# A hybrid decoder layer on one core: transfers that wait moved from SP's queue to POOL's, the residual spilled by chunks, and the fourth weight sum made last

## The chip, the core and the metric

The kernel runs on one core of a Trainium2 chip. Its time is the device time of one execution in microseconds (us); of several executions the median counts. The engines are TensorE (PE in the profile; its weight loads are PEld), VectorE (DVE), ScalarE (ACT), GpSimd (POOL) and SyncE (SP). Each engine works off its own instructions in order. DMAs are issued by SP (rows "SPq"), POOL ("POOLq") and ACT ("ACTq"); their packets appear in the profile under queue q1 (SP), q0 (POOL) and q10 (ACT), and all are carried by the core's 16 DMA engines.

## What is computed

One layer (DEPTH 1) of a decoder trunk on 512 positions of width 2048, in float32:

```
proj = rmsnorm(h) @ w_in                              # 2048 x 6672
ya = spatial gating MLP, 4 heads x 128;  yb = gated short convolution, 4 groups x 128
yc = gated DeltaNet, 8 heads x 128: short conv, silu, l2norm, a triangular solve by chunks, a scan
h = h + concat[ya, yb, yc] @ w_o
h = h + square(relu(rmsnorm(h) @ w_ff1)) @ w_ff2      # 2048 x 8192 and 8192 x 2048
h = h + (p @ w_ple_proj) * sigmoid(rmsnorm(h) @ w_ple_gate)
out = rmsnorm(h)
```

## The kernel before

Every large product is made of three matmuls: each operand is split into a high part (a cast by ACT, L181 and L276) and the rest (a subtraction by DVE, L182 and L277), and high x high, high x low and low x high are summed in PSUM. A weight tile is loaded by SP, split, and multiplied; tiles lie in a ring of SBUF (`place`, RING) and are loaded some slots ahead, since `wload` gives its instructions a high priority. The order of the instructions on each engine is made by a scheduler from such priorities.

The stages, by the time of the profile: the norm of x and the first columns of `w_in` (to 60 us); the spatial gating columns, with the decays of the heads made beside them in `prep` (to 140); eight heads (140 to 640), each with 16 weight loads and the generator `gdn` advanced between matmuls; four groups of the short convolution (to 780); `w_o` in two halves, of which `residual` adds blocks of 512 columns into the residual tiles `hs` (to 960); the up phase, `up_pairwise` for two groups of columns and `up_products` for thirty (to 1630); the down phase, seven calls of `product` (to 2260); gate, projection and final norm.

Up and down phase use fewer products than the plain form, at the price of sums. Of `w_ff2` four sums are made in DRAM, beside all else, by DMAs alone: `presum` yields one piece at a time. For each of 16 steps and each sum q0 to q3, SP copies a block of `w_ff2` to DRAM in four pieces (`copies`, L210), and POOL adds another block, or another sum, to it with accumulating DMAs (`adds`, L219). `count` is called for every weight load and draws pieces from the generator at `pace[1]` loads a piece:

```
def count(n=1):
    pace[0] += n
    while pace[1] and pace[0] >= pace[1]:
        pace[0] -= pace[1]
        next(sums, None)
```

In a head, `gdn` writes the products of k with themselves to DRAM (`at`, L600), reads their diagonal blocks back (`blk`, L602), has POOL invert these in a chain of small products into `tb`, and writes `tb` to DRAM (`td`, L645), from where `T` is read (L656). At its end the head's result `zs` goes to DRAM (`mix`, L733); after the second convolution group all eight are read back in pairs through one buffer `xs` (L795), and split. The residual is spilled before the large weight buffers `wp` take its place (`hsd`, L1032), and reloaded for the down phase (L1047). The up phase writes hidden rows to DRAM (`hd`, L979, issued by POOL), the down phase loads them (L1077) beside `w_ff2` or the sums (L1079).

Of the kernel before, what the change touches and what calls it, by code (L numbers as in the profile page):

```python
# [15 lines left out]
ALU = mybir.AluOpType  # L16
# [3 lines left out]
P = 128  # L20
S = 512
NT = S // P
# [36 lines left out]
def hybrid_block(ctx: ExitStack, tc: tile.TileContext, x, p, norm_mix, w_in, sg_ln_g, sg_ln_b, sg_w,  # L59
# [142 lines left out]
    def pieces(q, st, src):  # L202
        for b in range(2):
            for c in range(0, FW, 512):
                yield qd[q][st][:, b, c:c + 512], src[:, b, c:c + 512]

    def copies(i):
        for q, a, f in ((0, 0, 0), (2, 1, 1), (3, 1, 0), (1, 1, 1)):
            for dst, src in pieces(q, i, w2block(i, a, f)):
                tc.keep_in_program_order(nc.sync.dma_start(dst, src))  # L210
                yield

    def adds(i):
        for q, lag in ((0, 1), (2, 1), (1, 2), (3, 3)):
            st = i - lag
            if 0 <= st < NST:
                other = w2block(st, 0, 1) if lag == 1 else qd[0 if q == 1 else 1][st]
                for dst, src in pieces(q, st, other):
                    tc.keep_in_program_order(nc.gpsimd.dma_start(dst, src, accum_op=ALU.add))  # L219
                    yield  # L220

    def presum():
        for i in range(NST + 3):
            todo = [copies(i)] if i < NST else []
            todo.append(adds(i))
            while todo:
                for gen in list(todo):
                    try:
                        next(gen)
                    except StopIteration:  # L230
                        todo.remove(gen)
                        continue
                    yield
# [136 lines left out]
    pace[1] = 0.9  # L370

# [182 lines left out]
    if True:  # L554
# [32 lines left out]
        def gdn(c):  # L587
# [57 lines left out]
            nc.sync.dma_start(diag(td[h]), tb)  # L645
# [87 lines left out]
            nc.sync.dma_start(mixd[h], zs)  # L733
# [3 lines left out]
        gd = None  # L737
        for h in range(H):
# [42 lines left out]
        for gi in range(4):  # L781
            ps = [pd.tile([P, S], F32, name="d") for _ in range(3)]
            feature_major(col_blocks(w_in, [SC0 + 512 * i + gi * P for i in range(3)]), 3, KD, 2, ps)
            if gi == 1:
# [6 lines left out]
                for h in range(H):  # L791
# [3 lines left out]
                    nc.sync.dma_start(mt, mixd[h])  # L795
# [19 lines left out]
    def chain(*gens):  # L815
        for gen in gens:
            yield from gen
# [59 lines left out]
    def residual(c, ps, pool, nm, ss, g0, scale=None):  # L877
        for tt in range(NT):
            hc = accumulate(tt, c, ps[tt], scale)
            nc.scalar.activation(ps[tt], hc, AF.Square, accum_out=ss[:, tt, c:c + 1])  # L880
# [150 lines left out]
    for tt in range(NT):  # L1031
        nc.sync.dma_start(hsd[tt], hs[tt])  # L1032
# [5 lines left out]
    pace[1] = 1  # L1038
    for g in range(2, NG):
        up_products(g, *((pd, "d"), (pg, "g"))[g % 2])  # L1040
    for _ in sums:
        pass
# [194 lines left out]
```

## Time and profile before

| | |
|---|---|
| time, median of 3 runs (lowest, highest) | 2489.27 us (2488.5, 2491.82) |
| time of the profiled execution | 2482.61 us |
| its span, from the first to the last instruction | 2480.8 us |
| TensorE busy, share of the span | 2399.0 us, 97% |
| DVE, ACT, POOL busy | 60%, 43%, 16% |
| mean granted TensorE clock | 0.984 of full speed |
| moved by DMA | 508.91 MB, 205 GB/s; q1 52.4%, q0 20.7% of the 16 engines |

Durations in this document are from the profiled execution. A share of a DMA queue is the time that its packets took, as a share of all 16 engines over the stretch. A busy TensorE is not one at full speed: its granted clock stands beside the busy time, 1.00 at 2.4 GHz and 0.50 at 1.2 GHz.

### The profile page before, as it was taken

The page shows a single profiled execution, that of the slowest core. Times are in us where ns is not written, and L with a number is a line of the kernel's source. Part 1 is how long each engine was busy: PE and PEld are TensorE (multiplying, and loading weights), DVE is VectorE, ACT ScalarE, POOL GpSimd, SP SyncE. Part 2 cuts the span into 40 slices and gives each one's busy share as a digit, 9 for nine tenths or more (in the row PEclk, how much of TensorE's full clock was granted, in tenths as well). Part 3 has the DMA queues.
Part 4 walks back from the last instruction along what each step waited for, and adds up shares of the span by engine and source line. Part 5 has one row for each costly group of instructions (what it writes and reads, how often), then busy time and mean ns, then how long its engine had stood idle before and what let it go on. Part 6 is the DMA issues. An engine that isn't in the chain of part 4 may idle for free.

```text
span 2480.8 us, 35947 instructions
## 1 busy us (share of the span) xinstructions
PE 2399.0 (97%) x13852; PEld 2110.6 (85%) x13852; DVE 1488.5 (60%) x2047; ACT 1060.7 (43%) x1585; POOL 402.2 (16%) x613
## 2 busy tenths in 40 slices
PE   9999999999979999899999999989999999999998
PEld 8987888888857888899999999968888888888888
DVE  6654444444435357688888888855566565565334
ACT  5343333333323244344444444444444454455333
POOL 1433333333031100121222212310000000000000
PEclk9999999999989999999999999989999999999999
DMA  7976777776698946899889898988777777763333
GB/s 228 251 173 151 162 163 163 164 165 154 146 202 226 249 141 189 248 246 250 238 238 245 241 247 226 220 265 295 239 237 237 241 233 243 235 214 125 100 102 115
DMA packets 350175, 508.91 MB, mean 205 GB/s; under 512 B 38010, under 2 KB 218035, under 8 KB 348083
## 3 DMA queue, kind: packets, MB, share of 16 engines
q1 hardware_dynamic: 302436, 403.58, 52.4%
q0 software_dynamic: 44544, 96.49, 20.7%
q10 hardware_dynamic: 3024, 6.55, 0.8%
q8 instruction: 108, 1.77, 0.3%
q14 instruction: 63, 0.52, 0.1%
HBM read 460.11 MB, written 180.63 MB: 258 GB/s over the span
## 4 chain that ended last, share of the span: by engine, by line
PE 79%; DMA 9%; POOL 4%; DVE 3%; issue 2%; ACT 1%; SPq 1%; POOLq 0%; ACTq 0%; DVEq 0%
PE g L270 7%; PE g L271 7%; PE g L272 7%; PE d L270 7%; PE d L272 7%; PE d L271 7%; PE g L956 4%; PE g L957 4%; PE g L958 4%; PE d L957 4%; PE d L956 4%; PE d L958 4%; PE d L319 4%; PE d L320 4%; PE d L318 4%; DMA wraw<-in_w_in_dram 3%
## 5 line engine op out<-in xcount | busy, mean ns | idle before, releaser
L182 DVE TENSOR_TENSOR wl<-wraw,wh 128x512 fp32r<-128x512 f32 (+3 forms) x336 | 250.4, 748 | 364.6 <-ACT wh L181 356.3
L181 ACT CAST wh<-wraw 128x512 fp32r<-128x512 f32 (+3 forms) x336 | 216.9, 648 | 508.8 <-PE d L320 186.3
L318 PE MATMUL d<-XH,wh 128*128 128x512 f32 x704 | 296.9, 422 | 17.2 <-ACT wh L181 17.2
L319 PE MATMUL d<-XH,wl 128*128 128x512 f32 x704 | 278.8, 396 | 0.2 <-DVE wl L182 0.2
L320 PE MATMUL d<-XL,wh 128*128 128x512 f32 x704 | 278.5, 396 | 0.0
L1011 ACT CAST wh<-wp 128x1024 fp32r<-128x1024 f32 x140 | 147.2, 1051 | 197.5 <-PE g L958 99.3
L1012 DVE TENSOR_TENSOR wl<-wp,wh 128x1024 fp32r<-128x1024 f32 x140 | 170.9, 1221 | 54.8 <-ACT wh L1011 54.7
L277 DVE TENSOR_TENSOR wl<-wraw,wh 128x1024 fp32r<-128x1024 f32 x112 | 137.2, 1225 | 106.8 <-ACT wh L276 106.8
L277 DVE TENSOR_TENSOR r<-xr,r 128x1024 fp32r<-128x1024 f32 x112 | 136.8, 1222 | 77.0 <-ACT r L276 77.0
L276 ACT CAST wh<-wraw 128x1024 fp32r<-128x1024 f32 x112 | 118.2, 1055 | 141.3 <-PE d L272 72.7
L318 PEld LDWEIGHTS d<-XH,wh 128*128 128x128 f32 x704 | 134.7, 191 | 40.5 <-ACT wh L181 17.6
L270 PE MATMUL d<-wh,r 128*128 128x512 f32 x408 | 161.8, 397 | 4.8 <-ACT r L276 4.1
L271 PE MATMUL d<-wl,r 128*128 128x512 f32 x408 | 159.9, 392 | 0.0
L272 PE MATMUL d<-wh,r 128*128 128x512 f32 x408 | 159.7, 393 | 0.1
L320 PEld LDWEIGHTS d<-XL,wh 128*128 128x128 f32 x704 | 134.1, 190 | 29.6
L276 ACT CAST r<-xr 128x1024 fp32r<-128x1024 f32 x112 | 117.2, 1046 | 96.4 <-PE d L272 51.4
L319 PEld LDWEIGHTS d<-XH,wl 128*128 128x128 f32 x704 | 134.9, 192 | 23.6 <-issue 1.4
L219 POOL DMA_DIRECT2D q<-in_w_ff_dram x128 | 112.6, 1279 | 112.2 <-DMA q<-in_w_ff_dram 110.2
L270 PE MATMUL g<-wh,r 128*128 128x512 f32 x328 | 128.6, 392 | 0.0
L271 PE MATMUL g<-wl,r 128*128 128x512 f32 x328 | 128.2, 391 | 0.0
L272 PE MATMUL g<-wh,r 128*128 128x512 f32 x328 | 128.2, 391 | 0.0
L979 POOL DMA_DIRECT2D hd<-r x32 | 33.2, 1038 | 541.0 <-issue 352.7
(436 smaller groups left out, 6624.6 us busy)
## 6 DMA issues: line engine op xcount, KB each, us to landing
q<-in_w_ff_dram SPq DMA_DIRECT2D x256, 256.0 KB, 7.7
wp<-in_w_ff_dram SPq DMA_DIRECT2D x60, 1024.0 KB, 13.9
wraw<-in_w_in_dram SPq DMA_DIRECT2D x352, 128.0 KB, 4.8
q<-in_w_ff_dram POOLq DMA_DIRECT2D x128, 256.0 KB, 10.2
q<-q POOLq DMA_DIRECT2D x128, 256.0 KB, 11.0
wraw<-q SPq DMA_DIRECT2D x64, 512.0 KB, 4.3
xr<-q SPq DMA_DIRECT2D x64, 512.0 KB, 4.4
hd<-r POOLq DMA_DIRECT2D x32, 896.0 KB, 6.0
```

Source lines behind the costliest of these rows:

```text
L181: nc.scalar.copy(dst[0], rv)
L182: nc.vector.tensor_tensor(dst[1], rv, dst[0].bitcast(F32), ALU.subtract)
L270: nc.tensor.matmul(ps, ah, bh, start=start, stop=False)
L271: nc.tensor.matmul(ps, ah, bl, start=False, stop=False)
L272: nc.tensor.matmul(ps, al, bh, start=False, stop=stop)
L276: nc.scalar.copy(dh, src)
L277: nc.vector.tensor_tensor(dl, src, dh.bitcast(F32), ALU.subtract)
L318: nc.tensor.matmul(ps, wh[:, a, b], XH[:, k], start=k == 0, stop=False)
L319: nc.tensor.matmul(ps, wl[:, a, b], XH[:, k], start=False, stop=False)
L320: nc.tensor.matmul(ps, wh[:, a, b], XL[:, k], start=False, stop=k == nk - 1)
L956: nc.tensor.matmul(ps, wh, x[0], start=start, stop=False)
L957: nc.tensor.matmul(ps, wl, x[0], start=False, stop=False)
```

## The change

- The write of `td`, the write of `mix` and its eight reads are issued by POOL instead of SP.
- The spill of the residual, four DMAs of 1 MB by SP after `up_pairwise`, becomes sixteen of 128 x 512 by POOL, each issued in `residual` when its block is summed. The reload becomes sixteen of the same shape by POOL, drawn from a generator in the first product of the down phase.
- The sums q0, q2 and q1 are made in a first pass over the steps, q3 in a second. A piece is 64 rows by 1024 columns instead of 128 by 512; the number and size of pieces stay.
- Pieces are first drawn at the start of the heads (`pace[1]` is set there), in `up_products` at 1.2 loads a piece instead of 1, and what is left in the down phase at every other step of `product`; the rest after product 3. Product 5 is the reader of q3.

```
@@ -201,36 +201,45 @@
 
     def pieces(q, st, src):
         for b in range(2):
-            for c in range(0, FW, 512):
-                yield qd[q][st][:, b, c:c + 512], src[:, b, c:c + 512]
-
-    def copies(i):
-        for q, a, f in ((0, 0, 0), (2, 1, 1), (3, 1, 0), (1, 1, 1)):
-            for dst, src in pieces(q, i, w2block(i, a, f)):
-                tc.keep_in_program_order(nc.sync.dma_start(dst, src))
+            for r in range(0, P, P // 2):
+                yield qd[q][st][r:r + P // 2, b], src[r:r + P // 2, b]
+
+    def copies(q, st, a, f):
+        for dst, src in pieces(q, st, w2block(st, a, f)):
+            tc.keep_in_program_order(nc.sync.dma_start(dst, src))
+            yield
+
+    def adds(q, st, other):
+        if 0 <= st < NST:
+            for dst, src in pieces(q, st, other(st)):
+                tc.keep_in_program_order(nc.gpsimd.dma_start(dst, src, accum_op=ALU.add))
                 yield
 
-    def adds(i):
-        for q, lag in ((0, 1), (2, 1), (1, 2), (3, 3)):
-            st = i - lag
-            if 0 <= st < NST:
-                other = w2block(st, 0, 1) if lag == 1 else qd[0 if q == 1 else 1][st]
-                for dst, src in pieces(q, st, other):
-                    tc.keep_in_program_order(nc.gpsimd.dma_start(dst, src, accum_op=ALU.add))
-                    yield
+    def turns(gens):
+        gens = list(gens)
+        while gens:
+            for gen in list(gens):
+                try:
+                    next(gen)
+                except StopIteration:
+                    gens.remove(gen)
+                    continue
+                yield
+
+    def chain(*gens):
+        for gen in gens:
+            yield from gen
+
+    def b12(st):
+        return w2block(st, 0, 1)
 
     def presum():
-        for i in range(NST + 3):
-            todo = [copies(i)] if i < NST else []
-            todo.append(adds(i))
-            while todo:
-                for gen in list(todo):
-                    try:
-                        next(gen)
-                    except StopIteration:
-                        todo.remove(gen)
-                        continue
-                    yield
+        for i in range(NST + 2):
+            yield from turns([chain(*(copies(q, i, a, f) for q, a, f in ((0, 0, 0), (2, 1, 1), (1, 1, 1)) if i < NST)),
+                              chain(adds(0, i - 1, b12), adds(2, i - 1, b12), adds(1, i - 2, lambda st: qd[0][st]))])
+        for i in range(NST + 2):
+            yield from turns([chain(*(copies(3, i, 1, 0) for _ in range(i < NST))),
+                              adds(3, i - 2, lambda st: qd[1][st])])
 
     sums = presum()
     pace = [0, 0]
@@ -367,8 +376,6 @@
         nc.vector.tensor_copy(ab[:, tt], ps[:, 240:256])
         gelu(tt, ps, [(512, 240)])
     ahead[0] = AHEAD1
-    pace[1] = 0.9
-
     ps = pg.tile([P, P], F32, name="g")
     nc.tensor.transpose(ps[:, :nrows], rows[:nrows], ident[:nrows, :nrows])
     ccol = gs.tile([P, P], F32, name="ccol")
@@ -642,7 +649,7 @@
                 nc.gpsimd.tensor_tensor(pr[:, :m, :j + 1], blk[:, j, j + 1:].unsqueeze(2).broadcast_to([nb, m, j + 1]),
                                         tb[:, j, :j + 1].unsqueeze(1).broadcast_to([nb, m, j + 1]), ALU.mult)
                 nc.gpsimd.tensor_tensor(tb[:, j + 1:, :j + 1], tb[:, j + 1:, :j + 1], pr[:, :m, :j + 1], ALU.add)
-            nc.sync.dma_start(diag(td[h]), tb)
+            nc.gpsimd.dma_start(diag(td[h]), tb)
             while "v" not in f:
                 yield 1
             yield Y[4]
@@ -730,11 +737,12 @@
             ps = back(o)
             zs = f["z"]
             nc.vector.scalar_tensor_tensor(zs, ps.rearrange("q a b -> q (a b)"), gno, zs, ALU.mult, ALU.mult)
-            nc.sync.dma_start(mixd[h], zs)
+            nc.gpsimd.dma_start(mixd[h], zs)
             done[h] = True
 
         done = [False] * H
         gd = None
+        pace[1] = 0.9
         for h in range(H):
             c = {"h": h}
             ps = [pd.tile([P, S], F32, name="d") for _ in range(2)]
@@ -792,7 +800,7 @@
                     if h % 2 == 0:
                         mt2 = res.tile([P, 4, HS], F32, name="xs").rearrange("q (t a) b -> q t (a b)", t=2)
                     mt = mt2[:, h % 2]
-                    nc.sync.dma_start(mt, mixd[h])
+                    nc.gpsimd.dma_start(mt, mixd[h])
                     split(*mix(8 + h), mt)
             gen = short_conv(gi, ps)
             next(gen)
@@ -812,9 +820,6 @@
             nc.scalar.dma_start(t, x[tt * P:(tt + 1) * P])
             hs.append(t)
 
-    def chain(*gens):
-        for gen in gens:
-            yield from gen
     last = bg.pop()
     later(chain(last[0], load_residual()), last[1])
     XH = r1.tile([P, KD, S], F32R, name="XH")
@@ -877,6 +882,7 @@
     def residual(c, ps, pool, nm, ss, g0, scale=None):
         for tt in range(NT):
             hc = accumulate(tt, c, ps[tt], scale)
+            nc.gpsimd.dma_start(hsd[tt][:, c * 512:(c + 1) * 512], hc)
             nc.scalar.activation(ps[tt], hc, AF.Square, accum_out=ss[:, tt, c:c + 1])
 
         def rest():
@@ -1028,23 +1034,24 @@
     up_pairwise(1, pg, "g")
     spot[0] = 0
     drain()
-    for tt in range(NT):
-        nc.sync.dma_start(hsd[tt], hs[tt])
     hctx.close()
     wpp = hctx.enter_context(tc.tile_pool(name="wp", bufs=1))
     wp = [wpp.tile([P, KD, 256], F32, name=f"wp{i}") for i in range(2)]
     flat = hb.rearrange("q a b -> q (a b)")
     wide = [[ring[1 + i][:, :FW], ring[1 + i][:, FW:2 * FW], flat[:, i * FW:(i + 1) * FW]] for i in range(2)]
-    pace[1] = 1
+    pace[1] = 1.2
     for g in range(2, NG):
         up_products(g, *((pd, "d"), (pg, "g"))[g % 2])
-    for _ in sums:
-        pass
     hctx.close()
     hp = hctx.enter_context(tc.tile_pool(name="hp2", bufs=1))
     hs[:] = [hp.tile([P, D], F32, name=f"h{tt}") for tt in range(NT)]
-    for tt in range(NT):
-        nc.sync.dma_start(hs[tt], hsd[tt])
+
+    def reload():
+        for tt in range(NT):
+            for c in range(0, D, 512):
+                tc.keep_in_program_order(nc.gpsimd.dma_start(hs[tt][:, c:c + 512], hsd[tt][:, c:c + 512]))
+                yield
+
     nrf = res.tile([P, NT], F32, name="nrf")
     nc.vector.tensor_scalar(nrf, rf, -1.0, None, ALU.mult)
 
@@ -1078,6 +1085,10 @@
                     split(xh, xl, xr_)
                 nc.sync.dma_start(rv, wsrc(kp))
                 split(wh, wl, rv)
+            if m == 0 and kp >= 8:
+                next(loads, None)
+            if kp % 2:
+                next(sums, None)
             for t in range(2):
                 ts = slice(t * P, (t + 1) * P)
                 for f in range(2):
@@ -1102,7 +1113,10 @@
     def tmp(t, f):
         return uscr[:, 4 + 2 * t + f]
 
+    loads = reload()
     ps = product(0, 0, b2(0, 0))
+    for _ in loads:
+        pass
     for t, f in PAIR4:
         nc.scalar.copy(u(t, f), ps[t][f])
         add(t, f, ps[t][f])
@@ -1120,6 +1134,8 @@
         add(2 + t, f, u(t, f))
         add(2 + t, 2 + f, ps[t][f], -1)
         square(2 + t, 2 + f, ps[t][f])
+    for _ in sums:
+        pass
     ps = product(4, 1, b2(1, 0))
     for t, f in PAIR4:
         add(t, f, ps[t][f])
```

How the order of instructions changes at three places that the prediction speaks of. The first is SP's queue in the fifth head, from the write of `at` to the read of `T` (`wraw` are weight loads, `q` copies of the sums); before:

```order
L600 DMA at4_629<-AT_3887 128x4x128
L602 DMA blk_3890<-at4_629 32x16x16
L178 DMA wraw_69<-in_w_in_dram 128x2x128 x2
L591 DMA dec_4915<-dec6_623 128x512
L178 DMA wraw_69<-in_w_in_dram 128x2x128 x2
L645 DMA td4_637<-tb_3992 32x16x16
L210 DMA q0_5_148<-in_w_ff2_dram 128x512
L178 DMA wraw_69<-in_w_in_dram 128x2x128 x2
L656 DMA T_4317<-td4_637 128x4x128
```

and now:

```order
L607 DMA at4_629<-AT_3887 128x4x128
L609 DMA blk_3890<-at4_629 32x16x16
L178 DMA wraw_69<-in_w_in_dram 128x2x128 x2
L598 DMA dec_4915<-dec6_623 128x512
L178 DMA wraw_69<-in_w_in_dram 128x2x128 x2
L209 DMA q0_6_149<-in_w_ff2_dram 64x1024
L178 DMA wraw_69<-in_w_in_dram 128x2x128 x2
L663 DMA T_4317<-td4_637 128x4x128
L178 DMA wraw_69<-in_w_in_dram 128x2x128 x2
```

The write of td has left the queue, and three pairs of weight loads stand between blk and T, where two stood ahead of td and one behind it.

The second is after the last head (`ors` is the last small step of a head before its result `zs`). Before, on SP and then on POOL:

```order
L733 DMA mix7_1423<-zs_5791 128x512
L178 DMA wraw_69<-in_w_in_dram 128x2x128 x3
L795 DMA xs_6441<-mix0_1416 128x512
L795 DMA xs_6441<-mix1_1417 128x512
L178 DMA wraw_69<-in_w_in_dram 128x2x128 x3
L210 DMA q0_7_150<-in_w_ff2_dram 128x512
L795 DMA xs_6448<-mix2_1418 128x512
L795 DMA xs_6448<-mix3_1419 128x512
```

```order
L149 TENSOR_TENSOR ors_6362<-rs_ms_6363,mhalf_122 128x4
L219 DMA q3_3_194<-q1_3_162 128x512 x2
L219 DMA q0_6_149<-in_w_ff2_dram 128x512 x4
L219 DMA q2_6_181<-in_w_ff2_dram 128x512 x4
L219 DMA q1_5_164<-q0_5_148 128x512 x4
L219 DMA q3_4_195<-q1_4_163 128x512 x4
```

and now on POOL:

```order
L149 TENSOR_TENSOR ors_6362<-rs_ms_6363,mhalf_122 128x4
L215 DMA q1_6_165<-q0_6_149 64x1024
L740 DMA mix7_1388<-zs_5791 128x512
L803 DMA xs_6441<-mix0_1381 128x512
L803 DMA xs_6441<-mix1_1382 128x512
L803 DMA xs_6448<-mix2_1383 128x512
L803 DMA xs_6448<-mix3_1384 128x512
L803 DMA xs_6455<-mix4_1385 128x512
L803 DMA xs_6455<-mix5_1386 128x512
L803 DMA xs_6462<-mix6_1387 128x512
L803 DMA xs_6462<-mix7_1388 128x512
L215 DMA q1_6_165<-q0_6_149 64x1024 x3
L215 DMA q0_8_151<-in_w_ff2_dram 64x1024 x4
```

The write and the reads of mix now stand on POOL behind one add, and the adds that followed ors (16 and more) come after them.

The third is POOL's queue at the end of the up phase, around the last writes of hidden rows; before:

```order
L219 DMA q3_14_205<-q1_14_173 128x512
L979 DMA hd7_8207<-r2_8182 128x7x256
L219 DMA q3_14_205<-q1_14_173 128x512 x3
L219 DMA q3_15_206<-q1_15_174 128x512 x4
L979 DMA hd7_8207<-r2_8182 128x7x256
```

and now:

```order
L985 DMA hd7_8223<-r2_8194 128x7x256
L215 DMA q3_9_200<-q1_9_168 64x1024
L215 DMA q3_10_201<-q1_10_169 64x1024 x2
L985 DMA hd7_8223<-r2_8194 128x7x256
L215 DMA q3_10_201<-q1_10_169 64x1024 x2
L1052 DMA h0_15061<-hsd_6907 128x512 x2
L215 DMA q3_11_202<-q1_11_170 64x1024
L1052 DMA h0_15061<-hsd_6907 128x512 x2
L1052 DMA h1_15062<-hsd_6907 128x512 x2
L215 DMA q3_11_202<-q1_11_170 64x1024
L1052 DMA h1_15062<-hsd_6907 128x512 x2
L1052 DMA h2_15063<-hsd_6907 128x512 x2
```

Before, POOL ended the sums with seven adds around the last write but one; now three stand there, and the reload follows the last write with an add after every fourth chunk. Behind these rows POOL has 16 more adds of q3, and SP 13 copies of q3 among the loads of products 0 and 1.

## Rows read from the trace of the kernel before

**Rows 1.** Stretches: us, length, busy PE PEld DVE ACT POOL, PEclk, DMA, GB/s

```profile
80.00:100.00 20.00, 15.52 (x73) 14.70 (x74) 12.09 (x18) 11.41 (x22) 8.07 (x7) 0.83 0.93 276
200.00:220.00 20.00, 14.22 (x66) 11.62 (x65) 9.43 (x14) 7.14 (x13) 0.00 (x0) 0.83 1.02 271
240.00:640.00 400.00, 384.70 (x2056) 326.71 (x2055) 192.35 (x395) 143.00 (x367) 141.83 (x291) 0.99 0.70 160
700.00:740.00 40.00, 22.62 (x86) 17.44 (x86) 12.74 (x14) 8.72 (x13) 7.26 (x9) 0.74 0.96 216
...
960.00:1040.00 80.00, 67.14 (x486) 64.01 (x485) 54.95 (x103) 31.68 (x46) 9.71 (x11) 0.92 0.86 254
1620.00:1680.00 60.00, 48.62 (x225) 39.39 (x224) 29.49 (x31) 24.39 (x25) 8.01 (x9) 0.89 0.90 287
1100.00:1500.00 400.00, 400.00 (x3355) 400.00 (x3354) 329.54 (x380) 192.22 (x201) 80.19 (x90) 1.00 0.90 244
1740.00:2100.00 360.00, 360.00 (x1566) 293.58 (x1565) 215.72 (x195) 173.53 (x180) 0.00 (x0) 1.00 0.75 238
```

**Rows 2.** Waits of SP's queue: in total, times, longest

```profile
SPq L645 <- POOL tb L644: 83.7, 8, 15.9
```

**Rows 3.** Timeline of SP in a head: start, length, line, output, input

```profile
433.18 0.33 SPq L645 DMA_DIRECT2D td<-tb  x1
...
434.14 1.06 SPq L178 DMA_DIRECT2D wraw<-in_w_in_dram  x2
435.31 0.68 SPq L656 DMA_DIRECT2D T<-td  x1
```

**Rows 4.** Timelines of ACT and PE, same head; in brackets the wait before

```profile
443.79 0.62 ACT L181 CAST wh<-wraw 128x512 fp32r<-128x512 f32 x1 [4.27 <-DMA wraw<-in_w_in_dram]
...
444.63 0.49 PE L714 MATMUL g<-vw,inT 128*128 128x128 f32 x2 [2.36 <-ACT vw L697]
```

**Rows 5.** Timeline of POOL at the end of the last head

```profile
684.70 1.03 POOL L149 TENSOR_TENSOR ors<-rs_ms,mhalf 128x4 f32<-128x4 f32 x1 [50.06 <-DVE rs_ms L148]
```

**Rows 6.** DMA queues, 690 to 740 us: packets, MB, share

```profile
q0 software_dynamic: 2952, 5.36, 60.8%
q1 hardware_dynamic: 6491, 5.24, 38.0%
```

**Rows 7.** Timeline of ACT at the reads of mix

```profile
726.16 1.29 ACT L276 CAST r<-xs 128x512 fp32r<-128x512 f32 x2 [24.90 <-DMA wraw<-in_w_in_dram]
...
730.90 1.36 ACT L276 CAST r<-xs 128x512 fp32r<-128x512 f32 x2 [2.13 <-DMA xs<-mix]
```

**Rows 8.** Chain that ended last, start of the up phase: start, length

```profile
1017.14 16.89 DMA wraw<-in_w_ple_gate_dram
```

**Rows 9.** The same chain at the end of the up phase

```profile
1623.00 8.48 DMA q<-q
...
1650.86 9.86 DMA hd<-r
1660.79 3.60 DMA r<-hd
```

**Rows 10.** Timeline of ACT at the decays of the heads

```profile
86.42 0.60 ACT L469 ACTIVATE de<-g 128x512 f32<-128x512 f32 x1 [2.56 <-DMA dec<-de]
```

**Rows 11.** Timeline of POOL: four adds issued one after the other

```profile
433.16 3.36 POOL L219 DMA_DIRECT2D q<-q  x4
```

**Rows 12.** DMA issues: count, KB each, median us to landing

```profile
td<-tb SPq DMA_DIRECT2D x8, 32.0 KB, 1.7
```

**Rows 13.** DMA queue of SP, 1800 to 2100 us (down phase)

```profile
q1 hardware_dynamic: 19490, 70.95, 74.4%
```

**Rows 14.** DMA queue of POOL, 440 to 640 us (heads)

```profile
q0 software_dynamic: 4686, 8.52, 27.3%
```

**Rows 15.** DMA queues, 1100 to 1500 us (up phase)

```profile
q1 hardware_dynamic: 51684, 60.31, 45.7%
q0 software_dynamic: 14880, 36.71, 43.8%
```

## The prediction

> **What bounds the kernel now.** I read the busy time by stretches first, then the list of what SP waited for, then timelines and the chain of waits at the stretches that lose time, and last the shares of the DMA queues.
>
> TensorE sets the time. In the steady part of the up phase and of the down phase its matmuls fill the whole stretch at a granted clock of 1.00 (400.00 of 400 us, 360.00 of 360) [rows 1]. Nothing of the change touches the matmuls, so time can only come from stretches where TensorE stands or runs at the lower of its two clock levels. I take as the loss of a stretch its length less busy time times granted clock: 7.1 us (80 to 100), 8.2 (200 to 220), 19.1 (the heads, 240 to 640), 23.3 (700 to 740), 18.2 (960 to 1040) and 16.7 (1620 to 1680), 92.6 us in all [rows 1]. That is the ceiling.
>
> Why each stands:
> - **Heads.** SP issues in order. The write of a head's diagonal blocks (td) waits for POOL's chain of small products, 83.7 us over 8 heads [rows 2]. In the head at 412 us td goes out at 433.18, only then the next weight load at 434.14, then the read of T at 435.31 [rows 3]. That weight comes late, ACT waits 4.27 us for it, and the copy of vw that TensorE needs sits behind on ACT: TensorE stands 2.36 us [rows 4]. The reader should see that the weight itself is several slots ahead; it is ACT's order that passes the delay on.
> - **After the last head.** POOL had stood 50.06 us before the ors of the last head [rows 5] while SP's copies ran on, so the adds come in a burst: the software queue takes 60.8% of the DMA engines, SP's queue 38.0% [rows 6]. The write and the reads of mix go through that, on SP; ACT waits 24.90 us for the first pair of xs [rows 7] and TensorE with it.
> - **960 to 1040.** Four spills of 1 MB each of the residual stand among the weight loads of a stage that is 0.86 full on DMA [rows 1]. At its end a weight takes 16.89 us to land [rows 8].
> - **1620 to 1680.** The loads of the hidden rows wait for writes of hd, and these take 9.86 us beside adds and 1 MB reloads; the load behind it takes another 3.60 [rows 9].
> - **80 to 100.** ACT waits for the landing of dec (2.56 us, [rows 10]) among the first copies.
>
> **The change, part by part.** Base is the profiled execution, 2482.6 us (its span 2480.8).
>
> *Sums start with the heads.* Copies and adds leave 80 to 100, where DMA was 0.93 full. The wait for dec goes; POOL's own products for dec stay. Bounds 0 and 7.1; I take **4**, about half.
>
> *td on POOL, first head.* There are now six weight loads between blk and T on SP, far more than POOL's chain lasts. Bounds 0 and 8.2; I take **7**.
>
> *td on POOL, later heads.* SP no longer waits at td, but T is the next row that needs it, one weight load later. T can go when tb is done, plus POOL's issue (3.36 us for 4, 0.84 each [rows 11]), plus the landing, which the trace shows for SP's td only (1.7 us [rows 12]); the far bound is the 9.86 of the hd write [rows 9]; I take 2, since td is small. So SP stands about 3 us longer than before and one load further on (a head has 16 loads in some 61 us, 3.8 each): of the 4.27 us that ACT waited, little more than 1 is surely won, more if the weight lands faster. Bounds 0 and 19.1; I take **6**. Behind the POOL write stand only adds, which nothing reads before the down phase.
>
> *mix on POOL.* The order puts mix7's write and the eight reads of mix straight behind one add, ahead of the burst. The reads then start as zs is done, and SP's weights have no wait at all. What stays is the chain of pairs through one xs buffer: load, cast on ACT, next pair; in the trace ACT waits 2.13 us at the second pair [rows 7]. Three weight slots cover that. Bounds 2 (if only that second wait is saved) and 23.3; I take **19**, since the one wait that makes the loss is 24.90. The 24 issues that POOL gains here and at td cost 24 x 0.84 = 20 us of POOL, which has 50 us of idle in one piece there [rows 5]; if that idle were gone, mix would be late by an add or two. The new wait of mix on zs holds only adds.
>
> *Spill by chunks.* 12 of 16 chunks leave with the first three blocks of columns, before 960, only the last four beside the up phase's first loads. 3/4 of 4.2 MB at 3.15 us a MB (74.4% of 300 us for 70.95 MB [rows 13]) are 9.9 us of DMA taken out of a stretch that is 0.86 full. The copies ahead of the late weight stay (8 in place of 10). Bounds 3 and 18.2; I take **11**.
>
> *Reload by chunks on POOL.* SP loses four 1 MB loads between 1620 and 1700, and POOL issues 3 adds instead of 7 behind the last hd write but one. The wait of hidden rows for hd remains; I take the hd write and the load behind it back by some 3 us each and the first late weight with them. Bounds 0 and 16.7; **7**.
>
> *Sums in the second phase.* At 1.2 loads a piece the up phase leaves 13 copies and 20 adds, which the order puts into the products 0 and 1 of the down phase. An add costs 6.41 us of all engines a MB (27.3% of 200 us for 8.52 MB [rows 14]), 1.68 a piece, if rows of 4 KB change nothing; at best 0.82, as a plain copy [rows 13]. A product lasts 88.3 us (384 matmuls, 1566 in 360 us [rows 1]) and its own loads fill 74.4%, 65.7 us. Product 0 then holds 65.7 + 13.2 (reload) + 12 adds (20.2) + 8 copies (6.6) = 105.7, product 1 65.7 + 8 adds (13.4) + 5 copies (4.1) = 83.2: 188.9 against 176.6, 12.3 too much; with cheap adds 171.7, nothing too much. I take **8 lost**, nearer the upper end, since its row is the same operation. In the up phase fewer pieces win nothing: TensorE is full there already.
>
> *Pieces of 64 rows by 4 KB* are as many and as large as before; I put them at nothing beyond the bound just given.
>
> Sum: 4 + 7 + 6 + 19 + 11 + 7 - 8 = 46, so 2436.6 by the profiled execution. The median of the runs, 2489.27, stands 6.7 above that execution; the forecast is **2443 us**.
>
> **The rivals.**
> 1. *T takes td's place.* The wait on POOL only moves one row down, and the adds behind td slow the next weight as now. For it: the 3 us above. Against it: one load more is out. The 6 and the 7 go: 2456.
> 2. *After the last head it is bandwidth, not order.* The two queues hold 98.8% of the engines there [rows 6]; if the adds that precede ors still fill them, mix lands late from whichever queue. Only 5 of the 19 remain: 2457. Against it: in the order one add, no burst, stands between ors and mix7. The Trainium skill (page "DMA: Bandwidth & Descriptors", section "Issuing engines are not separate DMA queues") says that DMAs started by any engine run on the same 16 DMA engines and that another issuer saves only sequencer time; by that rule this rival is the case wherever the engines are full. The trace agrees in part: the engines are full there, but what ACT waited for stood behind others in SP's order.
> 3. *The start is not delayed.* The counter of loads runs on while its pace is 0, so the 33rd load releases 33/0.9 = 36 pieces at once: 18 copies and 18 adds, 18 x 0.82 + 18 x 1.68 = 45 us of DMA. Two heads (122 us) that are 0.70 full [rows 1] have 37 to spare: 8 lost, and the 7 of the first head: 2458.
> 4. *Slower: the software queue starves the weights.* Place: wherever POOL's queue now holds a backlog, above all products 0 and 1. It holds 13.2 + 20 x 1.68 = 46.8 us of work there; at a share of 60.8% that lasts 77 us, in which SP's weights get 38.0% [rows 6] in place of 74.4% [rows 13], so TensorE loses 36.4/74.4 of 77, 38 us. The same holds back mix, spill and reload, so 19, 11 and 7 go: 2482.6 - 17 + 38 + 6.7 = 2510. It decides once the shares under backlog are those of rows 6. Against it: in the up phase 43.8% and 45.7% stand beside each other [rows 15] and TensorE loses nothing. The Trainium skill (the same page, "DMA: Bandwidth & Descriptors", section "Queues, rings and completion order") says that each DMA engine serves the rows that have work by turns, packet by packet; with half the engines for each the loss would be 31 us and the time 2503. No run so far shows the two rows both backlogged beside these loads.
>
> **How the numbers follow.** Forecast 0.48; rival 1 0.13; rival 2 0.12; rival 3 0.08; two of these three at once 0.07 (about 2470); all three with the dear price of the sums 0.04 (about 2489, no change); rival 4 0.08. A measurement of this kernel can tell about 0.2%, 5 us, from no change. Faster 0.88, same 0.04, slower 0.08. The range reaches down to 85% of the 92.6 us with no price for the sums (2410, taken as 2412) and up past two rivals at once, to 2474.
>
> **What would show it.** Right: SP's wait on POOL at td gone and a shorter one at T; ACT's 24.90 us before xs under 5; 700 to 740 at a clock near 1.00; a weight at the end of 960 to 1040 that lands in under 10 us; TensorE at over 95% in product 0. Wrong: T waiting as long as td did, a software queue near 60% in the down phase with ACT waiting for weights, or a new idle stretch of TensorE in products 0 and 1. The prediction fails as a whole if the down phase loses over 40 us or if the stretch at 700 keeps its loss.

## The result, and the profile after

| | before | after |
|---|---|---|
| median of the runs (lowest, highest) | 2489.25 us (2488.5, 2491.82) | 2451.95 us (2450.17, 2452.51) |
| profiled execution, its span | 2482.61, 2480.8 us | 2451.52, 2449.8 us |
| TensorE busy; mean granted clock | 2399.0 us; 0.984 | 2393.1 us; 0.990 |
| DMA packets | 350175 | 313826 |

The ratio is 0.9847 (95% interval 0.983 to 0.9864): faster by some 38 us (31 us between the two profiled executions). The forecast, 2443 us, is 9 us below the median and the result lies in the range. The reasons behind it did far worse than the number, as the experiments show.

Stretches of the changed kernel (columns as in [rows 1]: start and end, length, busy PE, PEld, DVE, ACT, POOL, PEclk, DMA share, GB/s):

```profile
80.00:100.00 20.00, 20.00 (x113) 19.70 (x112) 16.94 (x29) 12.46 (x24) 6.88 (x5) 1.00 0.56 156
120.00:140.00 20.00, 17.02 (x65) 12.29 (x64) 10.14 (x19) 5.85 (x10) 6.70 (x7) 0.92 1.02 275
200.00:220.00 20.00, 16.71 (x93) 14.38 (x92) 8.68 (x13) 4.71 (x8) 4.82 (x7) 0.91 1.03 250
240.00:640.00 400.00, 396.85 (x2153) 338.21 (x2152) 199.99 (x402) 147.85 (x373) 147.32 (x298) 1.00 0.68 166
700.00:740.00 40.00, 30.71 (x123) 23.91 (x122) 15.39 (x16) 9.67 (x14) 12.96 (x17) 0.87 1.02 225
920.00:1000.00 80.00, 70.27 (x493) 65.39 (x492) 58.23 (x115) 33.16 (x51) 11.63 (x15) 0.96 0.79 225
1580.00:1660.00 80.00, 65.85 (x306) 54.05 (x305) 35.99 (x37) 30.09 (x31) 21.46 (x31) 0.89 0.91 300
1660.00:1860.00 200.00, 200.00 (x871) 163.15 (x870) 116.16 (x101) 97.00 (x97) 9.35 (x12) 1.00 0.85 274
```

Against [rows 1]: the stretch at 80 is full, the heads nearly so, the stretch at 700 is better but far from full, and two places are new or worse: 120 to 140, and the end of the up phase (it ends some 35 us earlier now, so 1580 to 1660 answers to 1620 to 1680 of before). The down phase is full from 1660 on.

What SP waited for in the heads (in total, times, longest), the answer to [rows 2]:

```profile
SPq L663 <- DMA td<-tb: 73.2, 8, 11.9
```

SP stands nearly as long at T as it stood at td (73.2 us, 83.7 before). Yet TensorE is nearly full. So a long wait of SP does not by itself cost the time; the run with the new shape alone, below, shows it with the wait at td itself.

To compare kernels, I sum over slices of 20 us what a slice loses (20 less busy time times granted clock, as in the prediction, there over longer stretches). The span less these sums is 2385 to 2391 us for all kernels below, so the table holds the differences to within a few us. The times of the experiments are ratios to the kernel before, run on the same chip. The changed kernel was timed only beside four runs of the kernel before with a median of 2489.25 us; in the sessions of the other runs that median was 2483.6 to 2485.0. Against those the changed kernel's 2451.95 us would be a ratio of 0.987. So a difference of some 0.2% (5 us) between the row "after" and the others says nothing.

| kernel | ratio, 95% interval | start 60-180 | first head 180-240 | heads 240-640 | after heads 640-800 | spill 800-1100 | end of up 1560-1720 |
|---|---|---|---|---|---|---|---|
| before | 1 | 7.7 | 8.2 | 20.5 | 23.9 | 18.4 | 17.1 |
| after | 0.9847 (0.983-0.9864) | 4.3 | 5.5 | 4.7 | 12.4 | 12.5 | 21.4 |
| **one part alone, on before** | | | | | | | |
| td on POOL | 0.9921 (0.9901-0.994) | 6.5 | 8.2 | 4.7 | 21.6 | 20.1 | 16.7 |
| mix on POOL | 0.9982 (0.9969-0.9996) | 8.2 | 8.0 | 16.9 | 15.6 | 21.2 | 20.2 |
| later start | 1.0009 (0.9992-1.0025) | 9.0 | 12.7 | 14.5 | 21.1 | 19.4 | 16.9 |
| spill by chunks | 0.9979 (0.9964-0.9995) | 7.7 | 8.3 | 24.4 | 20.4 | 14.5 | 19.1 |
| 64 x 1024 pieces | 0.9861 (0.9847-0.9876) | 2.6 | 8.7 | 4.3 | 21.3 | 11.4 | 14.5 |
| **after, one edit** | | | | | | | |
| 128 x 512 pieces | 0.9954 (0.9938-0.9969) | 14.8 | 11.6 | 7.6 | 8.5 | 15.9 | 22.4 |
| spill on ACT | 0.9838 (0.982-0.9855) | 5.1 | 5.0 | 2.2 | 12.2 | 9.9 | 18.3 |
| reload on ACT | 0.9852 (0.9834-0.9869) | 3.7 | 6.1 | 6.0 | 12.6 | 12.0 | 18.6 |
| counter reset | 0.9841 (0.9826-0.9855) | 0.7 | 6.9 | 5.1 | 10.2 | 11.7 | 18.8 |
| pause after heads | 0.9837 (0.9819-0.9855) | 4.8 | 5.1 | 3.8 | 8.5 | 10.0 | 19.9 |
| quiet end of up, reload on ACT | 0.9824 (0.9809-0.9839) | 6.7 | 5.7 | 2.1 | 11.2 | 11.6 | 13.4 |
| all of these | 0.9809 (0.9789-0.9829) | 0.7 | 5.6 | 3.9 | 5.8 | 11.6 | 11.2 |

Equal stretches of kernels that do the same thing there differ by up to 4 us (the heads of "before" and of "spill by chunks", 20.5 and 24.4; the heads of "spill on ACT" and "reload on ACT", 2.2 and 6.0); a smaller difference in one pair of runs says nothing.

### The profile page after: what moved, and what is told of

It reads as the page before. It is cut to its first block, busy times and chain, and to the rows that moved or that the text cites. A ratio compares the mean times of both kernels' runs of the same rounds, so it can differ in the third digit from the quotient of the medians.

```text
span 2449.8 us, 36101 instructions
## 1 busy us (share of the span) xinstructions
PE 2393.1 (98%) x13852; PEld 2106.3 (86%) x13852; DVE 1491.1 (61%) x2047; ACT 1060.0 (43%) x1585; POOL 428.2 (17%) x669
## 2 busy tenths in 40 slices
DMA packets 313826, 508.94 MB, mean 208 GB/s; under 512 B 34298, under 2 KB 214323, under 8 KB 312755
## 3 DMA queue, kind: packets, MB, share of 16 engines
q0 software_dynamic: 32256, 109.34, 21.3%
## 4 chain that ended last, share of the span: by engine, by line
PE 85%; DMA 6%; issue 4%; DVE 2%; POOL 1%; ACT 1%; SPq 0%; POOLq 0%; ACTq 0%; DVEq 0%
PE d L279 7%; PE d L280 7%; PE d L281 7%; PE g L280 6%; PE g L281 6%; PE g L279 6%; PE d L329 5%; PE d L327 5%; PE d L328 5%; PE d L963 4%; PE d L962 4%; PE d L964 4%; PE g L963 4%; PE g L964 4%; PE g L962 4%
## 5 line engine op out<-in xcount | busy, mean ns | idle before, releaser
L215 POOL DMA_DIRECT2D q<-q x128 | 110.1, 1097 | 101.7 <-DMA q<-in_w_ff_dram 96.1
```

## The experiments

### One part of the change at a time

`td` alone, on the kernel before:

```
-            nc.sync.dma_start(diag(td[h]), tb)
+            nc.gpsimd.dma_start(diag(td[h]), tb)
```

> The kernel before with one edit: the write of td on POOL's queue. Between before and after the heads (200 to 640 us) lose 18.8 us less (28.6 to 10.2, by length less busy time times granted clock). Theory A, SP free of td is the whole of it: 2470 to 2475 us, SP's wait moved to T and nearly as long, TensorE full in the later heads. Rival B, T takes td's place and the heads' gain in after comes from elsewhere (other pieces, other order of adds): 2485 to 2492 us. My sum had 6 for the later heads and 7 for the first, 2476.

Measured 0.9921, some 20 us (15 by the medians, 2483.58 and 2468.59), and it is theory A: the later heads lose 4.7 in place of 20.5. The first head keeps its 8.2. SP's waits in this kernel:

```profile
SPq L656 <- DMA td<-tb: 78.2, 8, 10.8
```

My rival 1 had the mechanism right, T takes td's place, but it doesn't decide: one weight load more had gone out ahead of the wait. ACT's longest wait for a weight at 240 to 640 falls from 7.1 to 3.8 us. That the one load is the reason is argued, not shown.

`mix` alone: `nc.sync` to `nc.gpsimd` at its write and its reads.

> The kernel before with one edit: the write and the reads of mix on POOL's queue. Theory A, it is SP's order that held mix and the weights: the loss at 700 to 740 (23.2 us) falls to about the 12.4 that after shows, 2478 us, and ACT's 24.9 us before xs goes. Rival B, the burst of adds sets it wherever mix is issued: the loss stays over 18, 2484 to 2492 us. My term of 19 would give 2470.

Measured 0.9982. After the heads 23.9 becomes 15.6, near theory A's 12.4. But the spill and the end of the up phase lose 2.8 and 3.1 us more, and the ratio leaves 4.5 us (1.5 by the medians): by the time it is rival B. What the 24.90 us of [rows 7] were is told by the chain that ended last, in the kernel before (start, length, what):

```profile
695.79 20.04 DMA mix<-zs
...
716.30 10.51 DMA xs<-mix
```

The write of mix took 20 us to land in the burst of adds, and the read behind it 10. On POOL's queue the write and the reads go out ahead of that burst.

The later start alone: `pace[1] = 0.9` set just ahead of the loop over the heads.

> The kernel before with one edit: the sums start with the first head, the counter of loads running on. Theory A, the early stretch is won (7.1 us at 80 to 100) and 36 pieces leave together at the first load of the heads, which costs 4 us there: 2484 to 2488 us. Rival B, the bunch hides: 2482 us. Rival C, the bunch costs more than the early stretch gives: over 2492 us.

Measured 1.0009, no change that can be told. The 7 us at 80 to 100 are won and the bunch takes them back at 120 to 240. That is rival 3 of the prediction.

The spill alone: sixteen chunks on POOL in `residual`, the four DMAs on SP taken out.

> The kernel before with one edit: the residual spilled by chunks on POOL's queue behind each block of columns. Theory A, the writes hold the adds behind them and let them go together, so the loss at 960 to 1040 (18.1 us) shrinks but a new one of some 5 to 7 us stands at the change to the up phase, as in after (12.6 us over both): 2482 to 2485 us. Rival B, the bytes are simply taken out of the full stretch: the whole 11 of my sum or more, 2472 to 2478 us.

Measured 0.9979, theory A by the time (0.9979 of 2489, 2484) and by the stretch (14.5).

### The shape of the pieces

First the changed kernel with the old shape:

```
-            for r in range(0, P, P // 2):
-                yield qd[q][st][r:r + P // 2, b], src[r:r + P // 2, b]
+            for c in range(0, FW, 512):
+                yield qd[q][st][:, b, c:c + 512], src[:, b, c:c + 512]
```

> The changed kernel with one edit: pieces of 128 rows by 2 KB again, as before. The sum had the shape at nothing. Theory A, the larger rows make an add cheaper (the software queue took 5.96 us a MB at 440 to 640 in after, 6.41 in before; 4.46 and 4.77 at 1100 to 1500), and where the engines are full this is time: 64 MB of adds at 0.4 us are 27 us of DMA, perhaps 5 us of it at the places where TensorE waits, ratio 0.987. Rival B, nothing: 0.9847.

Measured 0.9954: 27 us worse than the changed kernel by the ratios, 22 by the medians (2473.73 and 2451.95), four to five times theory A. Then the reverse, the kernel before with the new shape and nothing else:

> The kernel before with one edit: pieces of 64 rows by 4 KB in place of 128 by 2 KB. The changed kernel with the old pieces took 0.9954, so the shape is worth 26 us with the other edits. Theory A, it is worth as much alone, because every stretch that loses time is one where the engines are full and the cheaper copies and adds shorten each of those: ratio 0.989 to 0.993. Rival B, it pays only where the other edits make a burst (120 to 240: 26.4 us lost with the old pieces, 9.9 with the new): alone 0.997 to 1.000.

Measured 0.9861, more than theory A hoped for: **the shape alone gives 35 us, and the whole change 38**. By the medians the two kernels take the same time (2451.35 and 2451.95 us). The stretches of this kernel, and SP's wait:

```profile
80.00:100.00 20.00, 18.04 (x99) 17.36 (x98) 15.76 (x26) 12.47 (x26) 13.35 (x12) 1.00 0.80 222
240.00:640.00 400.00, 397.45 (x2156) 338.43 (x2154) 199.17 (x404) 148.16 (x373) 136.69 (x281) 1.00 0.69 167
680.00:720.00 40.00, 24.08 (x91) 18.65 (x90) 12.23 (x13) 8.71 (x13) 6.25 (x8) 0.79 0.91 219
940.00:1000.00 60.00, 54.19 (x398) 52.10 (x397) 45.84 (x94) 27.57 (x41) 9.40 (x11) 0.91 0.91 289
```

```profile
SPq L645 <- POOL tb L644: 82.3, 8, 15.9
```

SP waits at td just as in before (82.3 us, 83.7 in [rows 2]), and the heads lose 4.3 us instead of 20.5. Here the long wait is harmless. The likely reason is that the weights behind it land sooner: ACT waits 18.3 us for weights at 240 to 640, in before 31.3. td on POOL and the new shape remove the same 16 us; together they remove them once.

Why the shape matters is read from the queues. Before, over the whole span (packets, MB, share of 16 engines):

```profile
DMA packets 350175, 508.91 MB, mean 205 GB/s; under 512 B 38010, under 2 KB 218035, under 8 KB 348083
q1 hardware_dynamic: 302436, 403.58, 52.4%
q0 software_dynamic: 44544, 96.49, 20.7%
```

The same lines with the new shape alone:

```profile
DMA packets 317407, 508.91 MB, mean 208 GB/s; under 512 B 38010, under 2 KB 218035, under 8 KB 315315
q1 hardware_dynamic: 286052, 403.58, 51.9%
q0 software_dynamic: 28160, 96.49, 19.5%
```

The bytes are the same, the packets 32768 fewer: 65536 rows of 2 KB became 32768 of 4 KB, half in each queue. Share times span falls from 513.5 to 477.7 us for q0 and from 1299.9 to 1271.4 for q1, 64 us of all engines. (These shares are packet times added up; in full stretches they pass 1, as 1.02 and 1.03 above, so they are not quite the engines' busy time.) At 60 to 240, where q0 holds adds alone, the same 5.24 MB took 20.4% of 180 us before and 16.5% now:

```profile
q0 software_dynamic: 2880, 5.24, 20.4%
```

```profile
q0 software_dynamic: 1600, 5.24, 16.5%
```

That is 7.0 and 5.7 us a MB. By the table TensorE got 33 of the 64 us (95.7 lost before in these columns, 62.8 with the new shape). The Trainium skill (page "Perfetto Trace Analysis", section "DMA Optimizations") advises to batch small transfers, from 2 KB to 4 KB or 8 KB, where DMA is the limit. These runs agree (0.9861) if a transfer is read as a contiguous row: each DMA stayed at 256 KB. Whether the cheaper copies or the cheaper adds did it was not separated.

### What the changed kernel still loses

After the last head POOL holds its adds behind `ors`, the write and the reads of mix, and lets them go when the last read is issued (timeline of POOL, changed kernel: start, length, line, output, input; in brackets the wait before):

```profile
663.95 1.04 POOL L149 TENSOR_TENSOR ors<-rs_ms,mhalf 128x4 f32<-128x4 f32 x1 [43.34 <-DVE rs_ms L148]
...
672.14 0.59 POOL L740 DMA_DIRECT2D mix<-zs  x1 [6.34 <-DVE zs L739]
677.06 1.11 POOL L803 DMA_DIRECT2D xs<-mix  x2 [4.32 <-DMA mix<-zs]
...
695.35 1.06 POOL L803 DMA_DIRECT2D xs<-mix  x2 [5.22 <-DVE r L286]
696.40 2.49 POOL L215 DMA_DIRECT2D q<-q  x3
697.98 5.80 POOL L215 DMA_DIRECT2D q<-in_w_ff_dram  x6
```

In before the adds went out straight behind ors, which ended at 685.73 [rows 5]:

```profile
685.70 1.72 POOL L219 DMA_DIRECT2D q<-q  x2
686.82 7.34 POOL L219 DMA_DIRECT2D q<-in_w_ff_dram  x8
```

The casts of ACT in the changed kernel:

```profile
728.25 0.83 ACT L181 CAST wh<-wraw 128x768 fp32r<-128x768 f32 x1 [12.04 <-DMA wraw<-in_w_in_dram]
```

The reads of mix now come in time ([rows 7] had 24.90 us there), and a weight behind them is 12 us late. The burst now starts 31 us behind ors in place of at once; it did not go, it delays the weights of the next stretch instead. So the next run releases no pieces during the short convolutions (`pace[1] = 0` ahead of their loop, `pace[:] = 0, 0.9` behind it):

> The changed kernel with one edit: no copies and adds are released during the four short convolutions after the last head; those 36 pieces go to the down phase. After still loses 12.4 us from 700 to 740, where POOL lets 17 adds go in 22 us that stood behind ors and mix. Theory A, the burst is what is left of that loss: under 3 us there, and the down phase hides the pieces: ratio 0.981. Rival B, the loss there is the chain of mix through one buffer and the casts on ACT: 700 to 740 unchanged, 0.9847. Rival C, the down phase can't hide 36 more pieces: 700 to 740 full, products 2 to 4 under 97% busy, 0.985 to 0.99.

8.5 us are left of 12.4, a difference at the edge of what can be told: 13 adds released earlier still go out together from 694 us. Not all of theory A; rival C fell, the down phase stays full.

The counter of loads set to 0 where the sums start:

> The changed kernel with one edit: the counter of loads is set to 0 where the sums start, so no 36 pieces leave at the first load of the heads. After loses 9.9 us from 120 to 240. Theory A, my rival 3 (the start is not delayed, the burst only stands elsewhere) was at work and took back most of the early gain: 120 to 240 loses under 4 us, ratio to before 0.982. Rival B, the loss at 200 to 220 is the first head's own chain (td, T): only the 4.3 us at 120 to 140 go, 0.983. Rival C, what leaves there comes back in the down phase: 0.9847.

`pace[:] = 0, 0.9` in place of `pace[1] = 0.9`: the start, 120 to 140, falls from 4.3 to 0.7 (0.7 in the last run too, which has the same edit; 3.7 to 6.7 in the others on after with rows of 4 KB), the first head keeps 6.9, so rival B. What stands there in the changed kernel is T (timelines of POOL, SP and TensorE):

```profile
197.16 0.76 POOL L652 DMA_DIRECT2D td<-tb  x1 [0.36 <-POOL tb L651]
197.91 2.50 POOL L215 DMA_DIRECT2D q<-q  x3
199.50 4.91 POOL L215 DMA_DIRECT2D q<-in_w_ff_dram  x5
```

```profile
199.36 0.37 SPq L663 DMA_DIRECT2D T<-td  x1
```

```profile
204.47 0.72 PE L571 MATMUL g<-ident,T 128*128 128x128 f32 x4 [3.29 <-DMA T<-td]
```

Eight adds go out right behind td and share the engines with the read of T, which takes 5 us. In the run with the reset it is another wait: ACT stands 9.65 us for a weight, and behind it comes the silu of q (fq), which the profile names as what TensorE waited for:

```profile
196.06 0.63 ACT L181 CAST wh<-wraw 128x512 fp32r<-128x512 f32 x1 [9.65 <-DMA wraw<-in_w_in_dram]
```

```profile
205.60 2.04 PE L678 MATMUL g<-pr,U 128*128 128x128 f32 x8 [4.24 <-ACT fq L587]
```

The spill from ACT's queue (`nc.scalar` for `nc.gpsimd` in `residual`):

> The changed kernel with one edit: the sixteen writes of the spill are issued from ACT's queue, just ahead of the ACT instruction that reads the same chunk. After loses 12.6 us from 920 to 1000. Theory A, the adds wait behind the spills on POOL and then go out together, which makes the next weights late: with the spills elsewhere the adds go out one by one, 7 us of the 12.6 go, ratio to before about 0.982 (after: 0.9847). Rival B, it is the bytes of the spill: no change, 0.9847. Rival C, ACT loses its issue time on its own path to the casts (16 issues of some 0.5 us): slower, 0.987.

0.9838, and 9.9 us for 12.5: between theory A and rival B, and not told apart; it is not slower, so rival C fell.

The reload from ACT's queue (the same edit in `reload`):

> The changed kernel with one edit: the sixteen reloads of the residual are issued from ACT's queue, where they stand between the casts of product 0's weights and so leave one by one over the product, instead of all at once on POOL's queue before product 0 has its weights. After loses 21.4 us from 1580 to 1660, of which 10.9 us (1620 to 1660) lie where the reloads run. Theory A, the reload's 4.2 MB in 30 us make the weights late: those 10.9 us go, the 10.6 before them (the wait for the hidden rows) stay, ratio to before about 0.980. Rival B, the hidden rows and the adds set the whole: no change, 0.9847.

0.9852: rival B by the time. The end of the up phase loses 18.6, only 2.8 less. The chain of waits of the changed kernel there (start, length, what):

```profile
1585.07 5.19 DMA hd<-r
1590.53 7.65 DMA r<-hd
...
1616.28 14.50 DMA r<-hd
...
1634.33 16.53 DMA xr<-in_w_ff_dram
```

The hidden rows and weights behind them take 14.5 and 16.5 us to land, in slices (1620 to 1660) whose engines are 1.03 and 1.04 full. So the next run has the reload on ACT and keeps the sums away as well:

```
+        if g == NG - 2:
+            pace[1] = 0
...
-            if kp % 2:
+            if kp % 2 and (m or kp >= 16):
```

> The changed kernel, with no copies and adds released over the last two groups of the up phase and the first half of product 0, and the reload on ACT's queue. After loses 21.4 us from 1580 to 1660, with the reload on ACT 17.7. Theory A, the adds beside the last writes of the hidden rows make these, the reads of them and the weights behind late: under 8 us there, ratio to before 0.980. Rival B, it is the order of the buffers (the reads of the hidden rows can't start before the last writes have gone, and the writes take 5 us and the reads 7 with empty engines too): still over 14 us, 0.984.

13.4 us are left, 8.0 less than in the changed kernel and 5.2 less than with the reload on ACT alone; ratio 0.9824. Rival B is nearer by the stretch (it said over 14). By slices: at 1580 to 1600, where the first reads wait for the last writes, 7.3 us are left of 8.1; at 1600 to 1660, where the sums and the reload stood, 6.1 of 13.3. What is left in these is a load of hidden rows that still takes 20 us to land (chain of this run), in a slice (1620 to 1640) whose engines are 1.04 full without the sums released there:

```profile
1615.01 20.05 DMA r<-hd
```

### Put together

> The changed kernel with the edits that helped alone put together: the spill and the reload on ACT's queue, the counter of loads set to 0 where the sums start, no pieces released during the last head and the short convolutions, over the last two groups of the up phase and the first half of product 0; in exchange 0.85 loads a piece in the up phase in place of 1.2, and the last pieces before product 5 in place of product 4. Theory A, each loss is that of its own stretch and the up phase has room (0.80 full in after): 120 to 140 under 1 us, 700 to 740 under 4 (12.4 in after, 8.5 with the shorter pause), 920 to 1000 about 10, 1580 to 1660 about 12; sum some 28 us less than after, ratio to before 0.976 to 0.979. Rival B, bytes taken from one stretch come out in the next: the up phase, 0.93 full or more, falls under 100%, ratio 0.982 to 0.986.

2435.7 us, ratio 0.9809, the fastest of all and just clear of the changed kernel's interval. It lies between theory A (0.976 to 0.979) and rival B (0.982 to 0.986). Start and end are as theory A had them (0.7 and 11.2); after the heads 5.8 us are lost, where it said under 4, and around the spill 11.6, where it said about 10. A part comes back in the up phase (1.7 us) and around the spill (columns as before):

```profile
940.00:960.00 20.00, 13.41 (x84) 12.63 (x83) 14.69 (x33) 6.21 (x10) 0.00 (x0) 0.74 1.05 324
1100.00:1500.00 400.00, 398.30 (x3334) 397.69 (x3333) 326.30 (x376) 190.92 (x199) 90.86 (x106) 1.00 0.91 258
1700.00:2100.00 400.00, 400.00 (x1739) 326.20 (x1739) 237.94 (x213) 191.43 (x197) 18.70 (x24) 1.00 0.85 271
```

Its profiled execution is the fastest of its five: 2431.94 us, 3.8 below the median (highest 2444.88).

## Why the number was right and the reasons were not

**The step that failed** is "Pieces of 64 rows by 4 KB are as many and as large as before; I put them at nothing". They are as many, but each has half the rows, and rows cost time. Alone this gives 35 us. All else, on top of it, goes from 0.9861 to 0.9847, 3.5 us, with intervals that overlap, so it is not told from nothing. I had 46 us for it. The sum came out because the term that I left out was about as large as what I had put in too much; that is luck.

Point by point; "alone" is on the kernel before, "on top" is after against the new shape alone:

- **Sums start with the heads, 4.** Alone nothing (1.0009). On top the start loses 4.3 in place of 2.6. The wait for dec went as said; rival 3 took it back: the reset shows 3.6 us of it.
- **td, first head, 7.** Alone 0 (8.2 and 8.2). The bound was the loss of the stretch, but that loss belongs to no wait at td. On top 3.2, less than the 4 us that can be told.
- **td, later heads, 6.** Alone 15.8, so my value was too low: with one load of slack more nearly the whole loss went. On top nothing (4.3 and 4.7), since the new shape had already won it. Rival 1 was right about the wait and wrong about its price.
- **mix, 19.** Alone 8.3 in its stretch, on top 8.9. Rival 2 was half right: the reads came in time, the burst behind them did not vanish. The queues filled the engines, and I had counted the one wait that ended last as the whole loss. The row of the 24.90 us names a weight; that it was the first pair of xs, as I read it, is borne out only by the chain above.
- **Spill, 11.** Alone 3.9, at the edge of what can be told, on top nothing (11.4 and 12.5).
- **Reload 7 and sums in the second phase -8.** Together -1; on top the end of the up phase loses 6.9 more, -6.9. The price of sums and reload there is 8.0 by the quiet end, as large as forecast, though at the start of product 0 only: after 1660 nothing is lost. With both out of the way 13.4 are left, against 17.1 before and 14.5 with the new shape alone, so 1 to 4 us for the 7 of the reload's move off SP.
- **Rival 4** fell: no weight starves in products 1 to 4.

Of the signs that I named, three came: the wait at td gone, xs on time (ACT waits 4.32 us at most), and no late weight at the end of 960 to 1040:

```profile
1000.00:1040.00 40.00, 40.00 (x338) 40.00 (x337) 34.76 (x42) 20.43 (x22) 6.18 (x7) 1.00 0.81 228
```

One came hardly, a shorter wait at T (73.2 us for 83.7). Two did not: the clock at 700 to 740 (0.87), product 0 over 95% (at 1600 to 1700 TensorE is busy for 93 us at a clock of 0.93).

The rule that I weighed (the Trainium skill, page "DMA: Bandwidth & Descriptors", section "Issuing engines are not separate DMA queues") says that another issuer saves only the time to issue. With the new shape the runs agree in the sum only: all else on top is worth 3.5 us, not told from nothing. But that is a balance of stretches: the one with mix loses 8.9 us less, the end of the up phase 6.9 more. With the old shape td alone gave 20 us; there an order with a waiting head of the queue did matter.

Two lessons of method lie in this. The terms were bounded by the losses of their stretches one by one, and added; but a late weight has several causes, and removing any one of them wins the same time. And each edit of a change needs a price from a row. For the pieces the rows were there: 44544 packets of q0 that took 20.7% of the span.

The first head keeps its loss with td alone and with the shape alone (8.2 and 8.7 us). The traces show what stands there: ACT waits some 10 us for one weight, 10.36 in before, 9.93 with td alone, 10.50 with the shape alone:

```profile
200.85 0.62 ACT L181 CAST wh<-wraw 128x512 fp32r<-128x512 f32 x1 [10.36 <-DMA wraw<-in_w_in_dram]
```

In these three the weights issued at 185 to 200 us take 11.9 to 13.7 us to land in the median, and POOL has just let seven adds go behind the products for tb (in before at 187.53 to 193.45 us). That the adds are the cause is not shown: no run takes them away there and leaves the rest. How much of the spill's loss is the adds that wait behind it stays open too.

## What to carry to other kernels

Where DMA is nearly full, count rows before moving transfers between queues: the same bytes in rows of 4 KB instead of 2 KB gave here 35 us, and all else on top 3.5, not told from nothing (with the old rows one move alone, td, gave 20). A transfer that waits on a queue that also carries background work can turn that work into a burst behind it, so look for the burst as well as for the wait: after the heads the move of mix won 8 to 9 us, and 12.4 were left with the burst, 8.5 with a pause of the background work, 5.8 with the longer pause of the last run. And don't add up gains that remove the same wait.

## What the runs showed that I had not expected

- The same bytes in fewer rows took less packet time: 32768 rows fewer, 64 us of 16 engines less, an estimate of some 31 ns of one engine a row (64 x 16 / 32768). It is no fixed price: at 60 to 240, where adds and copies crowd, 1280 packets fewer in q0 saved 7.0 us, 88 ns each.
- SP may stand 82 us at td over eight heads, and TensorE loses 4.3 us at 240 to 640, the later seven.
- The new shape is worth 35 us where it is the only edit, and 27 us where it is the last (0.9954 to 0.9847; 22 by the medians).
